# A hybrid decoder layer on one core: the attention projection of the second token half moved into the last attention units, and the output projection begun with that half

## The chip, the cores and the metric

The kernel runs on one core of one Trainium2 chip. The metric is the device time of one execution in microseconds (us), a median of three runs. The core has a matrix engine (TensorE, PE in the profile), a vector engine (VectorE, DVE), an engine for activation functions (ScalarE, ACT), a general engine (GpSimd, POOL) and SyncE (SP), which here issues nearly all DMAs. Each engine carries out its own list of instructions in order; an instruction that waits holds up everything behind it on that engine.

## What is computed

One decoder layer over 1024 tokens of width 1024, in fp32. Cut to the part that the change touches:

```python
h = rmsnorm(x); hp = h @ w_in                          # s5 inputs, q, k, v, gates
y_ssm = s5_mixer(...)                                  # ends in a GLU
y_nsa = nsa_mixer(...)                                 # compressed + selected + window attention
gate = sigmoid(hp[..., o4:].reshape(b, s, 2, D_MODEL))
merged = gate[..., 0, :] * (y_ssm @ w_proj_ssm) + gate[..., 1, :] * (y_nsa @ w_proj_nsa)
x = x + merged @ w_out
h2 = rmsnorm(x)
x = x + square(relu(h2 @ w_up)) @ w_down               # MLP, d_ff 4096
```

## The kernel before, in words

Every large product is made in three matmuls: both operands are split into a high and a low part (h and l), and high times high, low times high and high times low are summed in PSUM (`mm3`, lines 76 to 78). A split is one ACT instruction for the high part and one DVE or POOL instruction for the low part. Data lie with channels in the 128 partitions and tokens along a row. Tokens are worked in two halves of 512, and a product of 512 input channels for one block of 128 output channels and one half is 12 matmuls of 128x512.

The work in order of time: input projection and state-space mixer (to about 440 us of the span), attention (440 to 771), the projection `pB` of the attention output (775 to 833), the output projection `wo` (833 to 914), then the MLP: 16 rounds of up products, each made of seven smaller ones (B11, T2, B21, T3, T1, B22, T4), and four groups of down products from about 1250.

**Attention.** There are 16 units: for head group 0 the query blocks 0 to 7 of 128 tokens, then for group 1 the blocks 7 down to 0. So the second token half (512 to 1023) is complete for all heads when unit 11 (counted from 0) has stored its output. A unit makes scores (`sS`, `sW`), a softmax spread over DVE, ACT and POOL, transposes of the probabilities (`ptp`), and value products (`op`); its output `ot` is stored to DRAM (`oD`). The scores of a unit are interleaved with the values of the unit before.

**Filler.** A generator, `glu_fill`, makes the gated linear unit of the other mixer (`gps`) and its projection (`pA`) in small steps of three matmuls, 104 steps for both token halves. `step_fill` runs 0.55 of such a step for each value step (`FILL`), and a whole one in the last two units. Each projected row is scaled by its gate (`ga`, loaded from `gD`) and stored to `pD` (lines 783 to 787). The filler's temporary tiles come from `g_tile`, which has two buffers for all names; its product takes one of the two PSUM tiles `S` that the scores use too.

**Tail.** After the last unit the attention pools are closed. O, the attention output of both halves, is loaded from `oD` (`os`) and split (`Oh`, `Ol`). For each of the two halves and 8 blocks, pB = 12 matmuls; the gate `gb` (tanh on ACT) scales it (one DVE instruction), `pa`, the row that the filler had stored, is added (another), and the sum is split into `Mh`, `Ml`. Then `wo`: for each of 8 output blocks, in the order 0, 4, 1, 5, 2, 6, 3, 7, 48 matmuls for both halves.

**Memory.** A pool of 40 buffers (B) and one of 16 (W) hold the operands of the tail and of the MLP. `big_tile` hands out W for the tiles numbered 16 to 31 (of each 56), which are M rows 0 to 3 and later the MLP operands T3 and T1. The raw down weights (`wd`, line 1229, 16 loads) are put in W too, so in the last up round they wait until T3 and T1 were read.

**What sets the order.** The framework orders each engine's instructions itself, by a timeline of its own, from the order in which the code states them; each buffer's reuse waits for its last reader.

Of the kernel before, what the change touches and what calls it, by code (L numbers as in the profile page):

```python
# [8 lines left out]
F32 = mybir.dt.float32  # L9
F32R = mybir.dt.float32r  # L10
I32 = mybir.dt.int32
AF = mybir.ActivationFunctionType
# [15 lines left out]
FILL = 0.55  # L28
# [10 lines left out]
def hybrid_block(ctx: ExitStack, tc: tile.TileContext, A, out):  # L39
# [749 lines left out]

    last = proj_tok(wa, 1, 0)  # L790
# [16 lines left out]
    fill = glu_fill()  # L807
    early = [6]
# [175 lines left out]
    for n, (g, i) in enumerate(order):  # L984
        due[1] = FILL if n < 14 else 1.0
        if g == 0 and i >= 3:
            next(pk, None)
            next(pk, None)
        if n + 2 < 16:
            load_q(n + 2)  # L990
        va = unit_scores(*order[n + 1], Ks[order[n + 1][0]]) if n + 1 < 16 else None
        vb = unit_values(st)
        st = interleave(va, 6, vb, i + 1 + min(i + 1, 5) + 2)
# [20 lines left out]
    def big_tile(name):  # L1014

        nbig[0] += 1
        return (wd_tile if 16 <= (nbig[0] - 1) % 56 < 32 else op_tile)(name)
# [89 lines left out]
    t1es = ExitStack()  # L1107
    t1p = pool("t1", t1es, side="right")
    PAIRS = [0, 4, 1, 5, 2, 6, 3, 7]
    Oh, Ol = big_rows("O", 4)  # L1110
    wpn = [ring.raw(A["wpn"][m]) for m in range(2)]
    for hf in (1, 0):
        for m0 in (0, 2):
            os_ = T_tile("os")
            for j, sl in enumerate(HALVES):
                SP.dma_start(out=os_[:, sl], in_=oD[m0 + j, :, HALVES[hf]])
                split(Oh[m0 + j][hf], Ol[m0 + j][hf], os_[:, sl], lo_eng=DVE)
    Mh, Ml = big_rows("M", 8)
    for m0 in (0, 4):
        ws = []  # L1120
        for hf in (1, 0):
            sl = HALVES[hf]
            for m in range(m0, m0 + 4):
                if hf:
                    ws.append(ring.blocks(wpn.pop(0) if wpn else ring.raw(A["wpn"][m])))
                pa = t1p.tile([128, 512], F32, tag="pa", bufs=4, name="pa")
                SP.dma_start(out=pa, in_=pD[m][:, sl])
                gb = t1p.tile([128, 512], F32, tag="gb", bufs=4, name="gb")
                SP.dma_start(out=gb, in_=gD[8 + m][:, sl])
                act(gb, gb, AF.Tanh, scale=0.5)  # L1130
                ps = B_tile("pB")
                mm512(ps, ws[m - m0], [t[hf] for t in Oh], [t[hf] for t in Ol], True, True)
                stt(gb, gb, 1.0, ps, ALU.add, ALU.mult)
                tt(DVE, gb, gb, pa, ALU.add)
                split(Mh[m][hf], Ml[m][hf], gb, lo_eng=DVE)
    t1es.close()

# [9 lines left out]
    NG = 16  # L1147

    H2.alloc(3)
    for n, m in enumerate(PAIRS):  # L1150
        SP.dma_start(out=X2[m], in_=A["xT"][m * 128:(m + 1) * 128, :])
        w = [ring.weights(half(A["wo"][m], i)) for i in range(2)]
        if n % 2:
            ps = [B_tile("wo") for _ in range(2)]
        else:
            s_ = S_tile("wo")
            ps = [s_[:, sl] for sl in HALVES]
        for i, hf in ((0, 1), (1, 1), (0, 0), (1, 0)) if n == 0 else ((0, 1), (0, 0), (1, 1), (1, 0)):
            mm512(ps[hf], w[i], [t[hf] for t in Mh[4 * i:4 * i + 4]], [t[hf] for t in Ml[4 * i:4 * i + 4]], i == 0, i == 1)
        for hf in (1, 0):  # L1160
# [9 lines left out]
            act(o[:, sl], o[:, sl], scale=g2[:, m:m + 1])  # L1170
        if m == 3:
            H2.operands(3, X2[3], X2[7], H2.NAMES[:1])
        elif m > 3:
            H2.operands(m - 4, X2[m - 4], X2[m], H2.NAMES[m == 7:3])
# [281 lines left out]
```

## Time and profile before

| what | value |
|---|---|
| device time, median of 3 runs | 1571.67 us (1571.4 to 1574.04) |
| profiled execution: its own time, and its span | 1577.54 us, 1575.8 us |
| busy share of PE, DVE, ACT, POOL | 93%, 73%, 44%, 60% |
| granted PE clock, mean over the span | 0.97 |
| attention's last value product ends | 770.95 us |
| first matmul of pB, of wo, of the MLP | 774.82, 832.99 (steady), 914.36 us |

The span runs from the first to the last instruction; the 1.7 us around it belong to the execution's own time. PE is busy nearly throughout, so its idle stretches and the stretches at a lower clock are where time can be found; the last part of the attention and the start of the down projection are two of them.

### The profile page before, as it was taken

What the parts mean: (1) busy time and instruction counts of PE and PEld (TensorE: products, weight loads), DVE (VectorE), ACT (ScalarE), POOL (GpSimd) and SP (SyncE); (2) the same over time, 40 slices, a digit from 0 to 9 for tenths busy, and PEclk for the clock granted to TensorE, in tenths of its full rate; (3) what the DMA queues carried; (4) which work ended last, traced back from release to release, by engine and by line L of the source; (5) the groups of instructions that cost most, each with busy time, mean ns of one, the idle gap of its engine ahead of it and who ended that gap; (6) DMA issues with size and microseconds to landing.
All of it is one profiled execution on the core that took longest, in us unless ns stands there. A gap on an engine that the chain in (4) does not pass through costs nothing. (4 is left out here: it accounts for less than half of the span.)

```text
span 1575.8 us, 21400 instructions
## 1 busy us (share of the span) xinstructions
PE 1463.9 (93%) x7222; PEld 1220.7 (77%) x7222; DVE 1148.9 (73%) x1799; ACT 685.9 (44%) x1399; POOL 943.6 (60%) x825
## 2 busy tenths in 40 slices
PE   8689889999988999999799988999999889999999
PEld 6578878788886887888578867888888667787877
DVE  6356777632268788887574498987778999998965
ACT  6143442312157778878544452222222344444431
POOL 2564555433135544645223477998888668989883
PEclk9889999999989999999899999999999999999999
DMA  8654523344111222122565215332232342423202
GB/s 287 68 150 140 143 83 102 108 147 143 67 48 47 75 80 64 32 66 72 183 217 212 95 66 201 130 111 107 108 117 78 120 141 80 134 81 127 74 1 107
DMA packets 111103, 173.80 MB, mean 110 GB/s; under 512 B 23425, under 2 KB 44673, under 8 KB 110994
## 3 DMA queue, kind: packets, MB, share of 16 engines
q1 hardware_dynamic: 110994, 172.44, 34.6%
q8 instruction: 57, 0.93, 0.3%
q14 instruction: 52, 0.43, 0.1%
HBM read 124.15 MB, written 46.22 MB: 108 GB/s over the span
## 5 line engine op out<-in xcount | busy, mean ns | idle before, releaser
L81 POOL TENSOR_TENSOR wl<-raw,wh 128x512 fp32r<-128x512 f32 x128 | 184.6, 1450 | 169.7 <-ACT wh L96 165.7
L81 POOL TENSOR_TENSOR wl<-wd,wh 128x512 fp32r<-128x512 f32 x96 | 147.1, 1543 | 52.6 <-ACT wh L96 43.9
L96 ACT ACTIVATE wh<-raw 128x512 fp32r<-128x512 f32 x128 | 80.4, 629 | 164.3 <-PE wB L77 77.6
L96 ACT ACTIVATE wh<-wd 128x512 fp32r<-128x512 f32 x96 | 59.5, 626 | 112.8 <-POOL wd L81 42.0
L90 POOL TENSOR_SCALAR pS<-pS,rs 128x128 f32<-128x128 f32 (+7 forms) x64 | 48.3, 755 | 99.4 <-DVE rs L81 77.3
L76 PE MATMUL gt<-hTh,wmh 128*128 128x512 f32 x256 | 101.5, 397 | 0.0
L77 PE MATMUL gt<-hTl,wmh 128*128 128x512 f32 x256 | 101.3, 396 | 0.0
L78 PE MATMUL gt<-hTh,wml 128*128 128x512 f32 x256 | 101.2, 395 | 0.0
L81 DVE TENSOR_TENSOR pl<-ptp,ph 128x512 fp32r<-128x512 f32 x132 | 88.8, 686 | 14.5 <-ACT ph L96 13.5
L81 DVE TENSOR_TENSOR rr<-rr,rs 128x512 f32<-128x512 f32 x64 | 92.4, 1449 | 1.7
L96 ACT ACTIVATE ph<-ptp 128x512 fp32r<-128x512 f32 (+1 forms) x148 | 84.1, 587 | 14.8 <-PE ptp L900 14.0
L81 POOL TENSOR_TENSOR wl<-sum,wh 128x512 fp32r<-128x512 f32 x48 | 75.2, 1571 | 14.9 <-ACT wh L96 14.9
L81 POOL TENSOR_TENSOR wd<-wd 128x512 f32<-128x512 f32 x48 | 76.0, 1590 | 6.8 <-DMA wd<-in_wdn 5.5
L81 DVE TENSOR_TENSOR gt<-gt,rbc 128x512 f32<-128x512 f32 x32 | 22.0, 688 | 70.2 <-PE gt L78 63.7
L93 DVE SCALAR_TENSOR_TENSOR rr<-rr 128x512 f32<-128x512 f32 x64 | 71.3, 1117 | 1.8
L81 DVE TENSOR_TENSOR rr<-wT,rr 128x512 f32<-128x512 f32 x80 | 54.5, 684 | 21.8 <-PE wT L78 21.2
L96 ACT ACTIVATE wh<-sum 128x512 fp32r<-128x512 f32 x48 | 30.1, 629 | 89.3 <-PE wT L77 27.2
L96 ACT ACTIVATE pW<-pW,mx 128x64 f32<-128x64 f32 (+5 forms) x128 | 65.4, 515 | 4.2 <-DVE mx L855 4.0
L90 POOL TENSOR_SCALAR pW<-pW,rs 128x64 f32<-128x64 f32 (+5 forms) x128 | 65.4, 525 | 0.0
L891 PE MATMUL op<-ph,vs 128*128 128x512 f32 x132 | 61.2, 464 | 1.7 <-ACT ph L96 1.4
L81 POOL TENSOR_TENSOR wml<-wmr,wmh 128x512 fp32r<-128x512 f32 x32 | 42.9, 1346 | 28.2 <-ACT wmh L96 26.8
L893 PE MATMUL op<-pl,vs 128*128 128x512 f32 x132 | 55.7, 422 | 4.4 <-DVE pl L81 4.4
(626 smaller groups left out, 5077.1 us busy)
## 6 DMA issues: line engine op xcount, KB each, us to landing
raw<-in_wup SPq DMA_DIRECT2D x68, 256.0 KB, 2.6
wd<-in_wdn SPq DMA_DIRECT2D x64, 256.0 KB, 2.8
hD<-rr SPq DMA_DIRECT2D x26, 512.0 KB, 2.7
ru<-hD SPq DMA_DIRECT2D x18, 512.0 KB, 3.6
wmr<-in_wm SPq DMA_DIRECT2D x32, 256.0 KB, 3.0
gD<-gt SPq DMA_DIRECT2D x32, 256.0 KB, 2.1
xt<-in_x SPq DMA_DIRECT2D x16, 256.0 KB, 5.4
qkvD<-rw SPq DMA_DIRECT2D x32, 128.0 KB, 2.0
```

What stands on the lines that cost most here:

```text
L76: PE.matmul(out=o, lhsT=lh, rhs=rh, start=first, stop=False)
L77: PE.matmul(out=o, lhsT=lh, rhs=rl, start=False, stop=False)
L78: PE.matmul(out=o, lhsT=ll, rhs=rh, start=False, stop=last)
L81: e.tensor_tensor(out=o, in0=a, in1=b, op=op)
L90: e.tensor_scalar(out=o, in0=a, scalar1=s1, scalar2=s2, op0=op0, op1=op1)
L93: DVE.scalar_tensor_tensor(out=o, in0=a, scalar=s, in1=b, op0=op0, op1=op1)
L96: ACT.activation(out=o, in_=i, func=func, **kw)
L891: PE.matmul(out=op, lhsT=vv, rhs=ph, start=n == 0, stop=n == len(jobs) - 1)
L893: PE.matmul(out=op, lhsT=vv, rhs=pl, start=False, stop=False)
```

## The change

The filler goes on after its 104 steps, by 36 more: from unit 12 on it loads O of the second half (`os`), splits it (`Yh`, `Yl`), makes the 8 pB products of that half, scales them, adds the row of `pD` (`pa`) and stores the sum to `pD` again. So that it gets there, `FILL` goes from 0.55 to 0.75, and in units 12 to 15 1.4 steps run for each value step (`FILL2`). The tail loads the merged rows of the second half from `pD` (`mg`) and splits them, makes `wo` of that half for the blocks 0, 4, 1 and 5 around the 8 pB products of the first half, then `wo` of the first half for these four with weights that it kept, then the other four blocks for both halves. pB is 192 matmuls and wo 384, as before. The kept weights lie in W, and `big_tile` gives W to T2 and B21 in place of T3 and T1. Eight pieces of pB weights are loaded and split a second time.

```diff
@@ -25,7 +25,8 @@
 NH = 8
 NBC = dict(b=2, c=2)
 PERIOD = 6
-FILL = 0.55
+FILL = 0.75
+FILL2 = 1.4
 PB = 9
 CY = 4
 ATT = dict(op=("o", 1), b=("p", 3), c=("p", 3))
@@ -787,6 +788,29 @@
                 SP.dma_start(out=pD[m][:, sl], in_=ga)
                 yield
 
+        while not half1:
+            yield
+        wn = ring.weights(A["wpn"][0])
+        Yh, Yl = rows(glp, "Y", 4)
+        for m in range(4):
+            os_ = g_tile("os")
+            SP.dma_start(out=os_, in_=oD[m, :, sl])
+            split(Yh[m], Yl[m], os_, lo_eng=DVE)
+            yield
+        for m in range(8):
+            w = wn
+            if m < 7:
+                wn = ring.weights(A["wpn"][m + 1])
+            gb, pa = g_tile("gb"), g_tile("pa")
+            SP.dma_start(out=gb, in_=gD[8 + m][:, sl])
+            SP.dma_start(out=pa, in_=pD[m][:, sl])
+            act(gb, gb, AF.Tanh, scale=0.5)
+            ps = yield from prod("pB", w, Yh, Yl)
+            stt(gb, gb, 1.0, ps, ALU.add, ALU.mult)
+            tt(DVE, gb, gb, pa, ALU.add)
+            SP.dma_start(out=pD[m][:, sl], in_=gb)
+            yield
+
     last = proj_tok(wa, 1, 0)
     while active:
         bg()
@@ -982,7 +1007,9 @@
     for _ in range(5):
         st = next(va)
     for n, (g, i) in enumerate(order):
-        due[1] = FILL if n < 14 else 1.0
+        if n == 12:
+            half1.append(n)
+            due[1] = FILL2
         if g == 0 and i >= 3:
             next(pk, None)
             next(pk, None)
@@ -1014,7 +1041,7 @@
     def big_tile(name):
 
         nbig[0] += 1
-        return (wd_tile if 16 <= (nbig[0] - 1) % 56 < 32 else op_tile)(name)
+        return (wd_tile if 48 <= nbig[0] - 1 < 64 else op_tile)(name)
 
     def big_rows(name, n):
 
@@ -1104,37 +1131,7 @@
...
-    t1es = ExitStack()
-    t1p = pool("t1", t1es, side="right")
     PAIRS = [0, 4, 1, 5, 2, 6, 3, 7]
-    Oh, Ol = big_rows("O", 4)
-    wpn = [ring.raw(A["wpn"][m]) for m in range(2)]
-    for hf in (1, 0):
-        for m0 in (0, 2):
-            os_ = T_tile("os")
-            for j, sl in enumerate(HALVES):
-                SP.dma_start(out=os_[:, sl], in_=oD[m0 + j, :, HALVES[hf]])
-                split(Oh[m0 + j][hf], Ol[m0 + j][hf], os_[:, sl], lo_eng=DVE)
-    Mh, Ml = big_rows("M", 8)
-    for m0 in (0, 4):
-        ws = []
-        for hf in (1, 0):
-            sl = HALVES[hf]
-            for m in range(m0, m0 + 4):
-                if hf:
-                    ws.append(ring.blocks(wpn.pop(0) if wpn else ring.raw(A["wpn"][m])))
-                pa = t1p.tile([128, 512], F32, tag="pa", bufs=4, name="pa")
-                SP.dma_start(out=pa, in_=pD[m][:, sl])
-                gb = t1p.tile([128, 512], F32, tag="gb", bufs=4, name="gb")
-                SP.dma_start(out=gb, in_=gD[8 + m][:, sl])
-                act(gb, gb, AF.Tanh, scale=0.5)
-                ps = B_tile("pB")
-                mm512(ps, ws[m - m0], [t[hf] for t in Oh], [t[hf] for t in Ol], True, True)
-                stt(gb, gb, 1.0, ps, ALU.add, ALU.mult)
-                tt(DVE, gb, gb, pa, ALU.add)
-                split(Mh[m][hf], Ml[m][hf], gb, lo_eng=DVE)
-    t1es.close()
...
-    H2.alloc(3)
-    for n, m in enumerate(PAIRS):
-        SP.dma_start(out=X2[m], in_=A["xT"][m * 128:(m + 1) * 128, :])
-        w = [ring.weights(half(A["wo"][m], i)) for i in range(2)]
-        if n % 2:
-            ps = [B_tile("wo") for _ in range(2)]
-        else:
-            s_ = S_tile("wo")
-            ps = [s_[:, sl] for sl in HALVES]
-        for i, hf in ((0, 1), (1, 1), (0, 0), (1, 0)) if n == 0 else ((0, 1), (0, 0), (1, 1), (1, 0)):
-            mm512(ps[hf], w[i], [t[hf] for t in Mh[4 * i:4 * i + 4]], [t[hf] for t in Ml[4 * i:4 * i + 4]], i == 0, i == 1)
+    t1es = ExitStack()
+    t1p = pool("t1", t1es, side="right")
+    Oh, Ol = ([big_tile("O" + x) for _ in range(4)] for x in "hl")
+    Mh, Ml = big_rows("M", 8)
+
+    def wo_weights(m, keep):
+
+        w = []
+        for i in range(2):
+            t = ring.raw(half(A["wo"][m], i))
+            if not keep:
+                w.append(ring.blocks(t))
+                continue
+            h, l = wd_tile("woh"), wd_tile("wol")
+            split(h, l, t)
+            w.append(tuple(a[:].rearrange("p (k m) -> p k m", k=4) for a in (h, l)))
+        return w
+
+    def wo_mm(o, w, hf):
+        for i in range(2):
+            mm512(o, w[i], [t[hf] for t in Mh[4 * i:4 * i + 4]], [t[hf] for t in Ml[4 * i:4 * i + 4]], i == 0, i == 1)
+
+    def wo_out(m, hfs, ps):
+
+        for hf in hfs:
             o, sl = X2[m], HALVES[hf]
...
+    def merge(m, ps):
+
+        sl = HALVES[0]
+        pa = t1p.tile([128, 512], F32, tag="pa", bufs=2, name="pa")
+        gb = t1p.tile([128, 512], F32, tag="gb", bufs=2, name="gb")
+        SP.dma_start(out=pa, in_=pD[m][:, sl])
+        SP.dma_start(out=gb, in_=gD[8 + m][:, sl])
+        act(gb, gb, AF.Tanh, scale=0.5)
+        yield
+        stt(gb, gb, 1.0, ps(), ALU.add, ALU.mult)
+        tt(DVE, gb, gb, pa, ALU.add)
+        split(Mh[m][0], Ml[m][0], gb, lo_eng=DVE)
+
+    kept = {PAIRS[0]: wo_weights(PAIRS[0], True)}
+    for m in range(8):
+        if m % 2 == 0:
+            mg = T_tile("mg")
+        t = mg[:, HALVES[m % 2]]
+        SP.dma_start(out=t, in_=pD[m][:, HALVES[1]])
+        split(Mh[m][1], Ml[m][1], t, lo_eng=DVE)
+
+    def first_half(ms):
+
+        s_ = S_tile("wo")
+        for j, m in enumerate(ms):
+            SP.dma_start(out=X2[m], in_=A["xT"][m * 128:(m + 1) * 128, :])
+            if m not in kept:
+                kept[m] = wo_weights(m, True)
+            o = s_[:, HALVES[j]]
+            wo_mm(o, kept[m], 1)
+            wo_out(m, (1,), {1: o})
+
+    first_half(PAIRS[:2])
+    for m0 in (0, 2):
+        os_ = T_tile("os")
+        for j, sl in enumerate(HALVES):
+            SP.dma_start(out=os_[:, sl], in_=oD[m0 + j, :, HALVES[0]])
+            split(Oh[m0 + j], Ol[m0 + j], os_[:, sl], lo_eng=DVE)
+    first_half(PAIRS[2:3])
+    for m in range(8):
+        w = ring.weights(A["wpn"][m])
+        ps = B_tile("pB")
+        mg = merge(m, lambda: ps)
+        next(mg)
+        mm512(ps, w, Oh, Ol, True, True)
+        for _ in mg:
+            pass
+    first_half(PAIRS[3:4])
+    t1es.close()
+
+    for n, m in enumerate(PAIRS):
+        if n == 4:
+            H2.alloc(3)
+        if n < 4:
+            ps = {0: B_tile("wo")}
+            wo_mm(ps[0], kept[m], 0)
+            wo_out(m, (0,), ps)
+            continue
+        SP.dma_start(out=X2[m], in_=A["xT"][m * 128:(m + 1) * 128, :])
+        w = wo_weights(m, False)
+        if n % 2:
+            ps = [B_tile("wo") for _ in range(2)]
+        else:
+            s_ = S_tile("wo")
+            ps = [s_[:, sl] for sl in HALVES]
+        for i, hf in ((0, 1), (0, 0), (1, 1), (1, 0)):
+            mm512(ps[hf], w[i], [t[hf] for t in Mh[4 * i:4 * i + 4]], [t[hf] for t in Ml[4 * i:4 * i + 4]], i == 0, i == 1)
+        wo_out(m, (1, 0), ps)
         if m == 3:
             H2.operands(3, X2[3], X2[7], H2.NAMES[:1])
-        elif m > 3:
-            H2.operands(m - 4, X2[m - 4], X2[m], H2.NAMES[m == 7:3])
+        else:
+            for k in (0, 1) if m == 2 else (m - 4,):
+                H2.operands(k, X2[k], X2[k + 4], H2.NAMES[m == 7:3])
     pre = H2.first([A["wup"][j] for j in range(4)])
     H2.alloc(4)
     for n in H2.NAMES[3:]:
```

Three places show how the instructions move. The first is PE at the end of the attention. Before, the last filler product (`pA`) stands ahead of the last unit's transposes (`ptp`) and value products (`op`):

```order
L76 MATMUL pA_8059<-Gh_6523,wh_7998 128x512
L77 MATMUL pA_8059<-Gl_6527,wh_7998 128x512
L78 MATMUL pA_8059<-Gh_6523,wl_7997 128x512
L900 MATMUL ptp_8008<-c_ident_487,pS_7929 128x128
L900 MATMUL ptp_8020<-c_ident_487,pW_7930 128x128
L900 MATMUL ptp_8008<-c_ident_487,pS_7969 128x128
L900 MATMUL ptp_8020<-c_ident_487,pW_7970 128x128
L900 MATMUL ptp_8032<-c_ident_487,pW_7930 64x128
L900 MATMUL ptp_8032<-c_ident_487,pW_7970 64x128
L891 MATMUL op_7994<-ph_8013,vs0_4662 128x512
L893 MATMUL op_7994<-pl_8014,vs0_4662 128x512
```

In the changed kernel the last filler product is the eighth `pB`. The last two scores (`sS`, `sW`) of the last unit come behind it:

```order
L79 MATMUL pB_8235<-Yh_7517,wl_8107 128x512
L918 MATMUL op_8061<-pl_8181,vs1_4689 128x512
L845 MATMUL sS_8241<-kh0_4684,qT_8072 128x128
L846 MATMUL sS_8241<-kl0_4686,qT_8072 128x128
L925 MATMUL ptp_8268<-c_ident_487,pS_8120 128x128
L925 MATMUL ptp_8286<-c_ident_487,pW_8121 128x128
L925 MATMUL ptp_8268<-c_ident_487,pS_8150 128x128
L925 MATMUL ptp_8286<-c_ident_487,pW_8151 128x128
L916 MATMUL op_8061<-ph_8216,Vc_123 128x512
L925 MATMUL ptp_8295<-c_ident_487,pW_8121 64x128
L925 MATMUL ptp_8295<-c_ident_487,pW_8151 64x128
L845 MATMUL sW_8246<-kh1_4685,qT_8072 128x128
```

So the last scores, which stood ahead of the last filler products, now follow the last one, and no filler follows them.

The second is SP in the same stretch. Before, each filler product has one load (`ga`) and one store (`pD`):

```order
L707 DMA raw_7995<-in_wps 128x512
L783 DMA ga_8001<-gD_88 128x512
L916 DMA oD_83<-ot_7573 128x2x128
L787 DMA pD_87<-ga_7853 128x512
L783 DMA ga_8056<-gD_88 128x512
L916 DMA oD_83<-ot_7777 128x2x128
L787 DMA pD_87<-ga_8001 128x512
L916 DMA oD_83<-ot_7958 128x2x128
L787 DMA pD_87<-ga_8056 128x512
```

Now each has two loads (`gb`, `pa`) and one store, and with two buffers in `g_tile` the load of a `pa` follows the store of the row before:

```order
L805 DMA gb_7586<-gD_88 128x512
L806 DMA pa_7587<-pD_87 128x512
L811 DMA pD_87<-gb_7586 128x512
L805 DMA gb_7686<-gD_88 128x512
L708 DMA raw_7764<-in_wpn 128x512
L806 DMA pa_7687<-pD_87 128x512
L941 DMA oD_83<-ot_7758 128x2x128
L811 DMA pD_87<-gb_7686 128x512
L805 DMA gb_7770<-gD_88 128x512
L708 DMA raw_7846<-in_wpn 128x512
L806 DMA pa_7771<-pD_87 128x512
L811 DMA pD_87<-gb_7770 128x512
```

The load `pa_7687` takes the buffer of `gb_7586`, whose store stands three rows ahead of it; the load `gb_7686` takes that of `pa_7587`.

The third is the end of the attention on PE. Before, pB of both halves follows the last value product:

```order
L891 MATMUL op_7994<-ph_8013,vs0_4662 128x512
L893 MATMUL op_7994<-pl_8014,vs0_4662 128x512
L891 MATMUL op_7994<-ph_8025,vs1_4663 128x512
L893 MATMUL op_7994<-pl_8026,vs1_4663 128x512
L891 MATMUL op_7994<-ph_8037,Vc_123 128x512
L76 MATMUL pB_8190<-Oh_8102,wh_8182 128x512
L76 MATMUL pB_8216<-Oh_8102,wh_8208 128x512
L77 MATMUL pB_8190<-Ol_8104,wh_8182 128x512
```

Now it is the output projection of the second half, with kept weights (`woh`, `wol`):

```order
L916 MATMUL op_8264<-ph_8291,vs1_4689 128x512
L918 MATMUL op_8264<-pl_8292,vs1_4689 128x512
L916 MATMUL op_8264<-ph_8300,Vc_123 128x512
L77 MATMUL wo_8437<-Mh_8366,woh_8399 128x512
L78 MATMUL wo_8437<-Ml_8368,woh_8399 128x512
L79 MATMUL wo_8437<-Mh_8366,wol_8400 128x512
L77 MATMUL wo_8437<-Mh_8370,woh_8399 128x512
L78 MATMUL wo_8437<-Ml_8372,woh_8399 128x512
```

The first work after the attention thus reads merged rows (`Mh`, `Ml`), not O.

## Rows read from the trace of the kernel before

**Rows 1.** The page, part 1: busy time, share of the span, instructions.

```profile
PE 1463.9 (93%) x7222; PEld 1220.7 (77%) x7222; DVE 1148.9 (73%) x1799; ACT 685.9 (44%) x1399; POOL 943.6 (60%) x825
```

**Rows 2.** Windows: stretch, its length, busy time by engine, PE clock, DMA.

```profile
440.00:540.00 100.00, 87.17 (x498) 75.15 (x496) 76.53 (x233) 72.64 (x204) 50.03 (x78) 0.90 0.18 54
540.00:705.00 165.00, 160.08 (x950) 135.34 (x948) 142.73 (x320) 134.53 (x304) 88.22 (x107) 1.00 0.21 61
728.40:772.70 44.30, 38.47 (x224) 31.09 (x222) 29.98 (x100) 30.79 (x96) 15.38 (x34) 0.99 0.23 72
772.70:790.00 17.30, 12.60 (x38) 9.32 (x39) 9.81 (x14) 10.79 (x18) 5.89 (x5) 0.72 1.01 341
790.00:835.00 45.00, 43.44 (x190) 35.30 (x189) 32.00 (x42) 19.41 (x33) 12.11 (x9) 1.00 0.57 187
```

**Rows 3.** Timeline, SP: store of unit 11. Start, length, engine, line, operation.

```profile
728.42 0.37 SPq L916 DMA_DIRECT2D oD<-ot  x1
```

**Rows 4.** Timeline, PE: attention's last products, first pB and slow matmuls after it.

```profile
759.76 0.50 PE L76 MATMUL pA<-Gh,wh 128*128 128x512 f32 x1 [1.84 <-DVE mx L855]
...
766.83 0.27 PE L900 MATMUL ptp<-c_ident,pS 128*128 128x128 f32 x1
...
770.45 0.50 PE L891 MATMUL op<-ph,Vc 128*128 128x512 f32 x1 [0.22 <-DVE ph L81]
774.82 1.22 PE L76 MATMUL pB<-Oh,wh 128*128 128x512 f32 x2 [3.87 <-ACT Oh L96]
...
776.27 0.63 PE L78 MATMUL pB<-Oh,wl 128*128 128x512 f32 x1
...
778.40 0.62 PE L77 MATMUL pB<-Ol,wh 128*128 128x512 f32 x1
```

**Rows 5.** Timeline, PE: output projection in full stride, and the MLP's first product.

```profile
832.99 0.39 PE L77 MATMUL wo<-Ml,wh 128*128 128x512 f32 x1
...
835.94 0.39 PE L78 MATMUL wo<-Mh,wl 128*128 128x512 f32 x1
...
914.36 0.39 PE L76 MATMUL first<-B11h,wh 128*128 128x512 f32 x1
```

**Rows 6.** DMA issues, 690 to 772 us: count, KB each, median us to landing.

```profile
pD<-ga SPq DMA_DIRECT2D x7, 256.0 KB, 2.3
ga<-gD SPq DMA_DIRECT2D x6, 256.0 KB, 3.0
...
oD<-ot SPq DMA_DIRECT2D x6, 128.0 KB, 1.8
os<-oD SPq DMA_DIRECT2D x3, 256.0 KB, 4.4
```

**Rows 7.** Tile ga: its DMAs' times to landing over the whole span.

```profile
DMA to landing us min/median/max: 2.0/2.5/4.3
```

**Rows 8.** Timeline, ACT: tanh and high half; queue wait in brackets.

```profile
757.30 0.63 ACT L96 ACTIVATE ga<-ga 128x512 f32<-128x512 f32 x1 [1.96 <-DMA ga<-gD]
...
770.99 0.77 ACT L96 ACTIVATE ot<-op 64x256 f32<-64x256 f32 x2 [2.02 <-PE op L891]
```

**Rows 9.** Timeline, DVE: last window maximum, product with gate, value sum.

```profile
760.60 0.28 DVE L855 CUSTOM_DVE_ANT_0 pW<-sW,c_wbias 128x128 f32<-128x128 f32 x1
...
762.86 0.69 DVE L93 SCALAR_TENSOR_TENSOR ga<-ga,pA 128x512 f32<-128x512 f32 x1 [0.24 <-PE pA L78]
```

**Rows 10.** Timeline, POOL: last scaling of probabilities.

```profile
763.83 0.95 POOL L90 TENSOR_SCALAR pW<-pW,rs 128x128 f32<-128x128 f32 x3
```

**Rows 11.** Waits of PE, 1227 to 1304 us: total, times, longest.

```profile
PE dn L76 <- ACT wh L96: 5.9, 1, 5.9
PE dnb L78 <- POOL wl L81: 5.6, 1, 5.6
```

**Rows 12.** Waits of POOL, 1220 to 1260 us.

```profile
POOL wd L81 <- DMA wd<-in_wdn: 3.4, 1, 3.4
```

**Rows 13.** Windows: the start of the down projection.

```profile
1253.00:1280.00 27.00, 18.55 (x63) 14.71 (x64) 27.00 (x21) 13.80 (x26) 22.70 (x15) 0.75 0.06 20
```

More of the change, by code (lines that the diff above doesn't have):

```diff
@@ L807, in hybrid_block @@
     fill = glu_fill()
+    half1 = []
     early = [6]
@@ L1147, in hybrid_block @@
     NG = 16
-    H2.alloc(3)
-    for n, m in enumerate(PAIRS):
-        SP.dma_start(out=X2[m], in_=A["xT"][m * 128:(m + 1) * 128, :])
-        w = [ring.weights(half(A["wo"][m], i)) for i in range(2)]
-        if n % 2:
-            ps = [B_tile("wo") for _ in range(2)]
-        else:
-            s_ = S_tile("wo")
-            ps = [s_[:, sl] for sl in HALVES]
-        for i, hf in ((0, 1), (1, 1), (0, 0), (1, 0)) if n == 0 else ((0, 1), (0, 0), (1, 1), (1, 0)):
-            mm512(ps[hf], w[i], [t[hf] for t in Mh[4 * i:4 * i + 4]], [t[hf] for t in Ml[4 * i:4 * i + 4]], i == 0, i == 1)
-        for hf in (1, 0):
+    t1es = ExitStack()
[18 more added lines that the diff above has]
+        for hf in hfs:
             o, sl = X2[m], HALVES[hf]
```

## The prediction

> **What bounds the kernel now.** I read the busy shares first: PE 93% of the span, DVE 73%, ACT 44% [rows 1]. So a change pays only where PE stands idle or slow, or where something else ends a stretch last. The table by stretches shows where that is. From 440 to 540 us PE is idle for 12.8 of 100 us and its clock is 0.90; from 540 to 705 it is idle for 4.9 of 165; in the last four units 5.8 of 44.3; in the transition 772.7 to 790, 4.7 of 17.3 at clock 0.72, with the DMA engines full (share 1.01) [rows 2]. The timeline of PE then shows what ends these waits: 3.87 us between the attention's last product and the first pB, which waits for a split of O, and after it matmuls 0.426 us apart (776.27 to 778.40, five steps) [rows 4], where steady ones are 0.227 apart (832.99 to 835.94, thirteen steps) [rows 5].
>
> Two marks cut the affected stretch: the store of unit 11 at 728.42, from which the second token half is complete [rows 3], and the MLP's first matmul at 914.36 [rows 5]. Between them lie 185.9 us.
>
> **Before unit 11's store.** The filler's 288 matmuls of gps and pA were 240 ahead of this store and 48 behind it; now all 288 are ahead, and six of pB: 54 more. At 0.227 that is 12.3 us of PE. Of the 54, 24 come in units 0 to 4, 5.4 us beside 12.8 us of idle time [rows 2]; I take them as hidden. The other 30 come where 4.9 us are idle in 165; I take 2.0 as hidden. **Term: +4.9 us.** Bounds: +12.3, if PE's gaps are waits for DVE that move along with it; -5, if all fits and half of the time that the 0.90 clock cost comes back (0.90 means 20 of 100 us at half speed, some 10 us of work).
>
> **From unit 11's store to the MLP.** Here 48 matmuls go and 90 of pB come, but I don't think that PE sets the end. Each of the eight products has two loads and a store, through two buffers. The load of a `pa` takes the buffer of the row before, whose store must have landed: store 2.3, load 3.0 [rows 6], the sum on DVE 0.69 (no row shows this sum; I take it from the product with the gate, also DVE on 128x512) [rows 9]. So one round takes 6.0 us. The first: store of O 1.8 and load 3.0 [rows 6], split 0.63 + 0.69, gate load 3.0 into a buffer that the split frees, tanh 0.63 [rows 8], product with the gate 0.69: 10.4 us after unit 11's store. From the first to the eighth product with the gate: 0.7 + 6 x 6.0 + (3.0 + 0.63 + 0.69) = 41.0. The product holds one of the two PSUM tiles that the scores use, so the last window score waits for the eighth: four score matmuls 0.9; from the window's maximum to POOL's last scaling 760.60 to 764.78, 4.2 [rows 9, 10]; from the transpose at 766.83 to the end of the last value product, 770.45 + 0.50, 4.1 [rows 4]. No filler is left to lie beside these 9.2 us. Sum 60.6.
>
> To this comes waiting in DVE's queue, where each sum stands in line with the softmax: DVE is busy 29.98 of 44.3 us with 100 instructions, share 0.68, 0.30 us each [rows 2]; as an estimate 0.68 / 0.32 x 0.30 = 0.64 per round, 4.5 for seven. The attention ends 65.1 us after unit 11's store; before it was 42.5 (770.95 - 728.42).
>
> Then 0.77 for the copy of the output [rows 8] and three splits on ACT ahead of the first `wo`, 2.7 in all (bounds 0.8 and the 4.4 of before). The tail keeps 480 of its 576 matmuls: 109.0 us. Before, it took 139.5 from the first pB to 914.36, 8.7 more than 576 x 0.227. Now `wo` of two blocks, 10.9 us, covers the loads of O, but the X2 loads, 4 MB, come ahead of them; I take 5.0 lost, between 1.6 (what is idle after 790 now [rows 2]) and 8.7. Sum 65.1 + 2.7 + 109.0 + 5.0 = 181.8. **Term: -4.1 us.** Bounds: -15 (first rival) and +12 (second).
>
> The weights split a second time cost nothing here: ACT is busy 30.8 and POOL 15.4 of 44.3 us in the last units [rows 2], and these become longer. If ACT's share were not covered, 8 x 0.63 = 5.0.
>
> **At the start of the down projection.** The down weights wait for T2 and B21, in place of T3 and T1: two products of 12 matmuls earlier, 5.4 us. POOL waits 3.4 us there for such a load [rows 12], and PE 5.6 and 5.9 for splits behind it [rows 11]. But DVE is busy 27.0 of 27 us there [rows 13], so most of what PE gains may be given back. **Term: -2.7**, half of 5.4. Bounds -5.4, and +2 if the loads meet the last round's transfers.
>
> **Sum.** +4.9 - 4.1 - 2.7 = -1.9 us: no change that can be told (under 0.2%, 3.1 us, a measurement of this kernel can't tell). The profiled execution took 1577.54, which would become 1575.6; on the runs' median, 5.9 lower, 1569.8, say 1570.
>
> **A rule against it.** After 3.87 us of idle PE ran at the lower level, 1.2 GHz [rows 4]; after 1.84 us at 759.76 [rows 4] it did not, clock 0.99 over the last units [rows 2]. My sum has some 17 us idle there (65.1 less 48 of work), in eight gaps of about 2 us, and takes 2.4 GHz for granted. The Trainium skill, "TensorE: Matmul & The Clock Gate", "HAM oscillation — how this bites in real kernels", says that a kernel whose every tile's compute is shorter than the wait for its next data falls back to the slow clock at each tile. By that rule the sum would be that of the fourth rival below. The row of 1.84 us speaks against it, that of 3.87 us for it.
>
> **Rivals.**
> First, the chain of loads is hidden and PE sets the end. PE's work in the last units is 38.5 less 10.9 for the 48 matmuls, 27.6; with 90 x 0.227 = 20.4 and the 5.8 idle of before, 53.8 in place of 65.1. That is 11.3 less: -13.2 in all, 1558.5. It needs rounds of under 4.9 us with the queue; the fastest load took 2.0 [rows 7], so 2.3 + 2.0 + 0.69 just misses it. For it: loads of the gate are issued a round ahead, and I may have put the last score too strictly behind the eighth product.
>
> Second, the chain is longer. The slowest load of `ga` took 4.3 [rows 7] and loads of O 4.4 [rows 6]. Seven rounds with 1.3 more are 9.1, the first load 1.4: +8.6 in all, 1580. The place is the last four units, where scores wait for PSUM. It decides from 6.9 us a round on (6.64 is mine with the queue); from 7.4 the change is measurably slower.
>
> Third, nothing of the 54 earlier matmuls is hidden: 7.4 more, +5.5, 1577. For it: DVE and ACT are busy 76 and 73% from 440 to 540 [rows 2], so a unit may simply end later. Against it: they are not full.
>
> Fourth, the clock falls in the eight gaps. At 0.426 ten matmuls cost 2.0 us more, sixteen for eight gaps; PE's 17 us of idle time hide three quarters, so +4; with the tail's loss at 8.7 and 1 us in the last value products, +9 on the sum: +7, 1579.
>
> **Chances.** The forecast's case 0.38 (1564 to 1577), the first rival 0.27, second 0.19, third 0.11, fourth 0.05. Faster by over 0.2%: 0.13 of the forecast's case and 0.25 of the first rival, 0.38. Slower: 0.08 of the forecast's, 0.16, 0.09 and 0.04 of the others, 0.37. The rest, 0.25, is no change. The range reaches to the first rival at 1557, and to the second with part of the third at 1586.
>
> **What would show it.** The store of unit 11 near 733 (+4.9); the stores of `gb` about 6.6 us apart, and the SP queue's loads of `pa` behind them; PE waiting for DVE's product with the gate at scores of the last units; the last value product near 798, no pB between the scores and it; first `wo` 2.7 us later; the MLP's first matmul near 915; the two waits of PE at the down projection shorter by some 3 us in sum. It would be wrong if the stores come under 5 us apart or over 7.4, if unit 11's store moves by over 10 us or not at all, or if the down projection gives over 5 us.

## The result, and the profile after

The changed kernel takes 1588.52 us (median of 4, 1584.87 to 1592.69) against 1572.24 (median of 4): a ratio of 1.0107, 95% interval 1.0079 to 1.0135. It is slower; the forecast was no change, 1570, with a range up to 1586. Its profiled execution took 1584.87 us, span 1583.1. That is only 7.3 us more than the span before, since the stretch ahead of the attention, which the change doesn't touch, happened to be 8.5 us shorter in it (first score at 435.6 us in place of 444.1). So stretches are compared here from mark to mark.

The windows of the changed kernel (stretch, length, busy time of PE, PEld, DVE, ACT, POOL, granted clock, DMA share, GB/s) answer to [rows 2]:

```profile
440.00:540.00 100.00, 88.81 (x499) 75.45 (x498) 81.48 (x246) 78.76 (x219) 57.59 (x88) 0.93 0.21 68
540.00:705.00 165.00, 161.03 (x943) 136.31 (x941) 137.52 (x297) 129.13 (x285) 86.82 (x102) 1.00 0.25 78
723.80:792.10 68.30, 58.23 (x290) 45.43 (x290) 46.77 (x130) 40.90 (x116) 25.66 (x44) 0.93 0.42 141
792.10:815.00 22.90, 12.47 (x34) 7.29 (x35) 8.24 (x9) 9.86 (x19) 8.28 (x6) 0.70 1.03 395
815.00:919.80 104.80, 102.48 (x447) 83.50 (x448) 62.17 (x76) 49.20 (x82) 43.88 (x31) 1.00 0.40 138
```

The denser filler hardly changes the first two rows. The last four units now take 68.3 us (42.5 before), and 10 of them PE is idle. Worst is the fourth row: in the first 23 us of the tail PE works for 12.5, at clock 0.70, while the DMA engines are full.

The clock of the third row, 0.93, comes from two places. One is the end of the attention, below. The other is the third and fourth of the eight products: after a wait of 1.64 us PE starts the third, and soon its matmuls are 0.43 us apart. PE's timeline, and the window around:

```profile
739.87 0.50 PE L77 MATMUL pB<-Yh,wh 128*128 128x512 f32 x1 [1.64 <-DVE mx L880]
...
743.09 0.63 PE L77 MATMUL pB<-Yh,wh 128*128 128x512 f32 x1
743.52 0.63 PE L78 MATMUL pB<-Yl,wh 128*128 128x512 f32 x1
```

```profile
740.00:750.00 10.00, 8.32 (x27) 6.39 (x28) 5.27 (x12) 5.08 (x15) 3.51 (x3) 0.71 0.42 141
```

SP's timeline (start, length, engine, line, operation) gives unit 11's store [rows 3] and the first, second and last stores of the merged rows:

```profile
723.82 0.37 SPq L941 DMA_DIRECT2D oD<-ot  x1
...
736.13 0.32 SPq L811 DMA_DIRECT2D pD<-gb  x1
...
742.87 0.32 SPq L811 DMA_DIRECT2D pD<-gb  x1
...
784.88 0.32 SPq L811 DMA_DIRECT2D pD<-gb  x1
```

Eight stores lie 48.75 us apart, 7.0 a round. PE's timeline at the end of the attention (in brackets the wait ahead and what ended it) answers to [rows 4, 5]:

```profile
784.72 0.28 PE L890 MATMUL sW<-kcl,qT 128*128 128x64 f32 x1
787.48 0.33 PE L925 MATMUL ptp<-c_ident,pS 128*128 128x128 f32 x1 [2.48 <-POOL pS L91]
...
791.42 0.66 PE L916 MATMUL op<-ph,Vc 128*128 128x512 f32 x1
794.11 0.50 PE L77 MATMUL wo<-Mh,woh 128*128 128x512 f32 x1 [2.03 <-ACT Mh L97]
...
805.63 0.80 PE L77 MATMUL wo<-Mh,woh 128*128 128x512 f32 x1 [7.23 <-ACT Mh L97]
...
919.86 0.39 PE L77 MATMUL first<-B11h,wh 128*128 128x512 f32 x1
```

After six `wo` matmuls PE waits 7.23 us for a split of a merged row on ACT. ACT's timeline there, and after it SP's, show why:

```profile
797.01 0.63 ACT L97 ACTIVATE woh<-raw 128x512 fp32r<-128x512 f32 x1 [1.91 <-DMA raw<-in_wo]
804.43 0.63 ACT L97 ACTIVATE gb<-gb 128x512 f32<-128x512 f32 x1 [6.79 <-DMA gb<-gD]
804.97 0.61 ACT L97 ACTIVATE Mh<-mg 128x512 fp32r<-128x512 f32 x1
```

```profile
793.71 1.61 SPq L1206 DMA_DIRECT2D x<-in_xT  x3
...
797.66 0.33 SPq L1187 DMA_DIRECT2D gb<-gD  x1
```

The split stands behind the tanh of a gate that only a later product needs, and this gate's load stands behind three X2 loads of 512 KB.

At the start of the down projection PE's waits, 1215 to 1330 us, answer to [rows 11]:

```profile
PE dn L77 <- DVE acc L82: 9.6, 1, 9.6
PE dnb L77 <- DVE acc L82: 5.7, 3, 2.8
```

The two waits for weights are gone, and PE waits for DVE in their place. The weights were loaded earlier, as SP's timeline shows: the 16 loads begin 18.4 us ahead of the first down matmul (1239.29 us), where it was 9.0 before. The next group's loads `ru` follow later, behind four raw rows of hidden values:

```profile
1220.89 11.96 SPq L1308 DMA_DIRECT2D wd<-in_wdn  x16
1233.18 50.85 SPq L708 DMA_DIRECT2D raw<-hD  x4
1285.43 1.52 SPq L1315 DMA_DIRECT2D ru<-hD  x3
```

In the kernel before, two raw rows stood there:

```profile
1227.63 10.65 SPq L1229 DMA_DIRECT2D wd<-in_wdn  x16
1273.27 4.94 SPq L707 DMA_DIRECT2D raw<-hD  x2
1279.58 3.72 SPq L1236 DMA_DIRECT2D ru<-hD  x3
```

Against the first down matmul `ru` is 46.1 us later, 43.0 before. Against the MLP's first matmul it is the same, 365.6 and 365.2. Which of the two matters is a question for the experiments.

### The profile page after: what moved, and what is told of

It is laid out like the page before. It is cut to its first block, busy times and chain, and to the rows that moved or that the text cites. A ratio compares the mean times of both kernels' runs of the same rounds, so it can differ in the third digit from the quotient of the medians.

```text
span 1583.1 us, 21410 instructions
## 1 busy us (share of the span) xinstructions
PE 1470.2 (93%) x7222; PEld 1219.5 (77%) x7222; DVE 1159.1 (73%) x1799; ACT 689.5 (44%) x1407; POOL 956.6 (60%) x833
## 5 line engine op out<-in xcount | busy, mean ns | idle before, releaser
L82 POOL TENSOR_TENSOR wl<-wd,wh 128x512 fp32r<-128x512 f32 x96 | 143.2, 1503 | 63.3 <-ACT wh L97 60.5
L880 DVE CUSTOM_DVE_ANT_0 pS<-sS,c_cbias 128x128 f32<-128x128 f32 (+7 forms) x64 | 48.0, 750 | 16.0 <-PE sS L846 13.0
```

The costliest lines, as they stand in the source:

```text
L82: e.tensor_tensor(out=o, in0=a, in1=b, op=op)
L880: DVE.tensor_tensor_reduce(out=dst, in0=ps, in1=bias, scale=nsl, scalar=3e38, op0=ALU.add, op1=ALU.min, accum_out=mx[:, b, h:h + 1])
```

## The experiments

All stand against the kernel before, run beside them. The marks, from PE's and SP's timelines: the first score, unit 11's store, the end of the last value product, the first matmul of the tail (pB before, `wo` after), the MLP's first matmul, the first down matmul, the 97th of `dnb` (a sum of the down products; that matmul lies in the second of their four groups), and the end. Times in us; ratio of the whole to the kernel before.

| kernel | score to store 11 | to last value | tail's first to MLP | down to 97th dnb | MLP to end | ratio (95%) |
|---|---|---|---|---|---|---|
| before | 284.3 | 42.5 | 139.5 | 124.4 | 661.4 | 1 |
| changed | 288.2 | 68.3 | 125.8 | 128.4 | 663.2 | 1.0107 (1.0079 to 1.0135) |
| e1_fill75 | 289.0 | 33.1 | 135.4 | 124.5 | 661.7 | 1.0007 (0.9996 to 1.0019) |
| e2_pa_own | 290.2 | 65.1 | 124.3 | 126.7 | 661.3 | 1.0093 (1.0074 to 1.0112) |
| e3_tail_late | 290.0 | 70.1 | 114.2 | 126.2 | 661.2 | 1.0063 (1.0047 to 1.0078) |
| e4_w_t3t1 | 288.4 | 68.2 | 127.4 | 124.9 | 665.0 | 1.0134 (1.0113 to 1.0154) |
| e5_bank | 291.9 | 57.2 | 119.8 | 126.6 | 663.0 | 1.0061 (1.0036 to 1.0086) |
| e6_own_tail | 296.9 | 62.0 | 113.9 | 126.9 | 663.5 | 1.0071 (1.0047 to 1.0094) |
| e7_combo | 294.8 | 51.2 | 115.3 | 126.6 | 664.7 | 1.0013 (0.9997 to 1.0029) |
| e8_fill2_08 | 290.7 | 57.8 | 119.1 | 125.9 | 660.8 | 1.0125 (1.0090 to 1.0160) |
| e9_ru_first | - | - | - | - | - | 1.0183 (1.0161 to 1.0205) |
| e10_combo_ru | 297.6 | 55.5 | 114.8 | 130.9 | 668.0 | 1.0062 (1.0046 to 1.0077) |
| e11_bank_tail_ru | 290.0 | 57.6 | 114.9 | 131.0 | 669.3 | 1.0079 (1.0058 to 1.0099) |
| e12_before_bank | 293.3 | 41.2 | 135.5 | 124.2 | 662.9 | 0.9991 (0.9974 to 1.0007) |
| e13_combo_all | 317.8 | 53.7 | 115.5 | 127.7 | 664.4 | 1.0066 (1.0046 to 1.0086) |

How far one profile can be trusted: e10 differs from e7 only in loads of the down projection, yet its first two columns sum to 353.1 against 346.0. Differences under about 7 us in them are not read as effects.

**e1_fill75: the denser filler alone.**

```diff
-FILL = 0.55
+FILL = 0.75
```

> The kernel before with FILL 0.75 in place of 0.55, nothing else: the filler of 104 steps is done by unit 11, and the last four units have none. From the first score to the store of unit 11 it was 284.3 us before and 288.3 in the changed kernel. Theory A: the denser filler alone costs these 4 us, so about 288 here; and the last four units lose their 48 filler matmuls, 10.9 us of PE, of which the softmax chain lets only a part be gained: from the store of unit 11 to the last value product 36 to 39 us in place of 42.5. In all -1 to +1 us. Rival: unit 11 is late in the changed kernel because the pB part (weights, loads of O, six matmuls) is already mixed in before its store; then 285 to 286 here and the whole is 3 to 5 us faster.

Unit 11's store moved as in the changed kernel (+4.7 and +3.9 us), and the last units took 33.1, less than theory A's 36 to 39. Most of the 9.4 us that they gained was given back at once: PE then stands still for 10 us (3.9 before), until O is loaded and split. The two rows are the last units and this gap:

```profile
728.50:761.70 33.20, 30.59 (x188) 23.89 (x188) 29.05 (x105) 30.51 (x98) 16.66 (x38) 1.00 0.17 56
761.70:771.80 10.10, 0.00 (x0) 0.00 (x0) 0.84 (x2) 4.76 (x10) 5.12 (x5) 0.65 0.84 278
```

**e2_pa_own: own buffers for pa.** In e6, e7, e10 and e13 `gb` has such buffers too (tag Gl).

```diff
-            gb, pa = g_tile("gb"), g_tile("pa")
+            gb = g_tile("gb")
+            pa = gg[0].tile([128, 512], F32R, tag="Gh", bufs=4, name="pa")[:].bitcast(F32)
```

> The changed kernel, with four buffers of their own for the filler's pa (in tiles that the other mixer's projection has left), so that its load no longer waits for the store of the row before; all else as it was. Theory A (the two buffers set the pace of the last units): the rounds of pB shrink from 7.0 us to 4 or less where nothing else holds them, and from the store of unit 11 to the last value product it takes 54 to 58 us in place of 68; the whole 8 to 13 us faster than the changed kernel. Rival B (the last units are long because the scores wait for PSUM tiles and for DVE, whatever the loads do): 65 to 68 us there, and no gain over 3 us.

65.1 us: rival B. The window answers to the third row of the changed kernel, with the same idle time of PE and the same clock:

```profile
728.90:794.00 65.10, 56.18 (x290) 44.55 (x290) 45.43 (x130) 40.26 (x116) 25.07 (x44) 0.94 0.42 137
```

**e3_tail_late: the tail's other loads held back.**

```diff
+            tt(POOL, X2[m][:, 0:1], Mh[7][1][:, 0:1].bitcast(F32), Ml[7][1][:, 0:1].bitcast(F32), ALU.add)
             SP.dma_start(out=X2[m], in_=A["xT"][m * 128:(m + 1) * 128, :])
...
+        tt(POOL, pa[:, 0:1], ...)   # and gb, ahead of their loads in merge
```

> The changed kernel, in whose tail the loads of X2 and of pa and gb are made to wait until the last merged row of the second half (Mh, Ml of block 7) is split, by writing one column of their buffers from it; all else as it was. Theory A: the wait of 7.2 us of PE after six wo matmuls comes from ACT, which stands at the tanh of a gb whose load is behind 1.5 MB of X2, with the merged rows' splits queued behind it; so that wait goes, and from the first wo matmul to the MLP's first it takes 115 to 118 us in place of 125.8, the whole 7 to 10 us faster than the changed kernel. Rival B: the DMA engines are full from 794 to 820 in any case, and what is put later makes the residual sums and pB late instead: 122 to 126 us, and waits of PE for DMA-fed splits further on.

Theory A's number, and a little better: the tail takes 114.2 in place of 125.8 us. ACT's order has no tanh in it until the merged rows are split:

```profile
804.85 0.63 ACT L97 ACTIVATE woh<-raw 128x512 fp32r<-128x512 f32 x1 [1.23 <-DMA raw<-in_wo]
805.38 0.61 ACT L97 ACTIVATE Mh<-mg 128x512 fp32r<-128x512 f32 x1
```

All kernels with this edit lie at 113.9 to 115.5. The DMA engines are just as busy; what they carry first has changed. So the edit moves the bytes and the order on ACT together. For the order speaks the trace of the changed kernel: six loads of merged rows (`mg`) were issued there by 790.72 and took 8.4 us at most, and ACT stood at the tanh until 804.43.

**e4_w_t3t1: the old rule for W.**

```diff
-        return (wd_tile if 48 <= nbig[0] - 1 < 64 else op_tile)(name)
+        return (wd_tile if 64 <= nbig[0] - 1 < 80 else op_tile)(name)
```

> The changed kernel with the W buffers given to T3 and T1 again, as before the change, in place of T2 and B21. Theory A: the earlier down weights are what costs time at the start of the down projection, since SP then has a third raw row of hidden values, whose buffer is not free, ahead of the loads ru that the next group needs: with the old rule ru is issued first again, and from the first down matmul to the end it takes 339 us as before the change, in place of 343.8; the 2.8 us that the up rounds gained, mostly right after the first product, are lost or not, and the MLP's second product may wait for rows of M, whose buffers T2 and B21 now take (2 to 10 us). Rival B: the 4.6 us there are a spread between executions: 343 us again.

The number of theory A came nearly: 340.2 us from the first down matmul to the end (339.2 before, 343.8 in the changed kernel), and SP again issues two raw rows and then `ru`:

```profile
1241.57 10.36 SPq L1308 DMA_DIRECT2D wd<-in_wdn  x16
1287.21 4.93 SPq L708 DMA_DIRECT2D raw<-hD  x2
1293.52 3.71 SPq L1315 DMA_DIRECT2D ru<-hD  x3
```

But the first down matmul stands 324.8 us after the MLP's first here (319.4 in the changed kernel, 322.2 before), so that from the MLP's first to the end it is 665.0, no less than 663.2. What is won at one mark had been lost at another; e9 and e10 tell what sets both.

**e5_bank: pB in another PSUM bank.**

```diff
-            ps = S_tile(name)[:, 0:512]
+            ps = B_tile(name) if name == "pB" else S_tile(name)[:, 0:512]
```

> The changed kernel, with the filler's pB products in one of the three PSUM banks of the transposes in place of one of the two tiles of the scores; all else as it was. Theory C (the scores of the next unit wait for the PSUM tile that a pB holds until DVE has taken it, and everything in order behind them on PE waits too): with two tiles free for scores, from the store of unit 11 to the last value product it takes 56 to 62 us in place of 68.3, and PE's waits at scores for DVE go. Theory A (the loads and the store of the filler in two buffers): 66 to 69 us. Rival D (transposes and value products now wait for PSUM in their turn): 66 to 72 us, with waits at the transposes.

57.2 us: theory C's number, though PE's waits at scores were only 2.1 us in the changed kernel (1.0 now), and 2.7 at pB itself for the scores' maximum on DVE (none now); most went by another way. The last scores' row of the tile view (first and last start), of the changed kernel, then of this one, and its window:

```profile
L890 PE MATMUL sW<-kcl,qT x11: 272/276/277, 724.9 to 784.7; 128*128 128x64 f32 x11
```

```profile
L890 PE MATMUL sW<-kcl,qT x9: 272/277/278, 733.9 to 772.6; 128*128 128x64 f32 x9
```

```profile
732.60:789.80 57.20, 52.00 (x284) 41.79 (x284) 40.94 (x122) 39.00 (x110) 24.79 (x44) 1.00 0.46 148
```

The last score ran 7.4 us before the last value product ended (792.1), and now 17.2 us before (789.8): the last softmax lies beside products again, and the clock stays at 2.4 GHz. Over the first two columns, the five kernels with pB in a tile of the scores (e8 apart) need 355.3 to 360.1 us (mean 357.5), the four with the bank (e13 apart) 346.0 to 353.1 (mean 349.0): 8.5 us. At this mark own buffers differ by nothing that shows: 355.3 and 358.9 with, 356.5, 356.6 and 360.1 without; with the bank 346.0 and 353.1 against 349.1 and 347.6. The five have a clock of 0.89 to 0.95 in the last units, the four 1.00 (e10: 0.94); how much of the 8.5 us is order and how much clock, no run separates.

At the first `wo` it is otherwise. In e5 each `gb` load goes out right behind the store of the row before, by SP's timeline; the eight stores lie 6.4 us apart (e11: 6.5, forecast 6.6), and DVE's wait at the product with the gate is for the tanh on ACT, not for PE:

```profile
783.76 0.32 SPq L811 DMA_DIRECT2D pD<-gb  x1
784.12 0.43 SPq L805 DMA_DIRECT2D gb<-gD  x1
...
790.00 0.32 SPq L811 DMA_DIRECT2D pD<-gb  x1
```

```profile
DVE gb L94 <- ACT gb L97: 2.0, 3, 1.2
```

The last store leaves at 790.00, the loads of the merged rows begin behind it at 793.47, and the first `wo` comes 9.0 us after the last value product (2.0 in the changed kernel):

```profile
798.78 0.80 PE L77 MATMUL wo<-Mh,woh 128*128 128x512 f32 x1 [8.97 <-ACT Mh L97]
```

In the changed kernel this product waited for both, and in e7, with the bank and own buffers, for PE alone, with the stores 5.0 us apart:

```profile
DVE gb L94 <- ACT gb L97: 4.0, 4, 2.0
DVE gb L94 <- PE pB L79: 2.1, 2, 1.3
```

```profile
DVE gb L94 <- PE pB L79: 3.8, 3, 1.5
```

So two limits of nearly the same length lie side by side, the two buffers and the tile. From the first score to the first `wo` the five kernels without the bank need 357.3 to 362.1 us (mean 359.5), the bank alone 358.1 and 356.7 (e5, e11), both parts 348.1 and 355.2 (e7, e10). That e5 is faster as a whole than the changed kernel comes, by the profiles, from its tail, 119.8.

**e6_own_tail and e7_combo: parts together.** e6 has own buffers for gb and pa and the edit of e3; e7 the bank of e5 too.

> The changed kernel with four buffers each for the filler's gb and pa, and the tail's X2, pa and gb loads held until the last merged row is split (as tried apart before: pa alone gave 3.2 us in the last units, the held loads 11.5 in the tail). Theory C: without any wait for a store the last units still take 60 to 64 us from the store of unit 11, since PSUM and the order on PE stay; the whole 1576 to 1579. Theory A: 54 to 57 us and 1569 to 1572.

> Everything together: pB in a PSUM bank of the transposes, own buffers for gb and pa, and the tail's other loads held until the last merged row is split. Theory C: neither PSUM nor a store holds the last units, so they come down to PE's own work of 46 us and the 9 us of the last softmax: 53 to 58 us; the whole 1566 to 1572, at or below the kernel before. If the waits only change their place (rival D): 60 us or more, and 1575.

e6: 62.0 us in the last units, as theory C had it, but 296.9 ahead of them, and the whole at 1581.45, above both forecasts. e7: 51.2 us and 1572.70: the loss is gone, but nothing is won against the kernel before. Against e6, which lacks only the bank, the medians differ by 8.8 us. Its last units and its tail:

```profile
734.40:785.60 51.20, 47.89 (x271) 39.36 (x269) 40.62 (x112) 33.64 (x97) 24.64 (x43) 1.00 0.48 151
785.60:902.90 117.30, 113.42 (x481) 91.84 (x481) 70.77 (x80) 58.29 (x99) 59.65 (x61) 0.96 0.56 196
```

PE is busy 161 of 168.5 us. Yet from the first score to the last value product e7 needs 346.0, and e1, the same filler without pB, 322.1: 23.9 us for 96 matmuls that are worth 21.8 in the tail.

**e8_fill2_08: fewer products among the last units.**

```diff
-FILL2 = 1.4
+FILL2 = 0.8
```

> The changed kernel with FILL2 0.8 in place of 1.4: some three of the eight pB products stand after the last unit's own work in the program, or beside its last softmax. Theory C (each product among the last units costs more than its 2.7 us, since scores wait behind it): from the store of unit 11 to the last value product 50 to 60 us, and the products left over lie beside the last softmax, so that the MLP's first product comes 4 to 10 us earlier against the store of unit 11 than in the changed kernel (196.0). Rival: the merged rows of the second half come that much later, the output projection waits for them, and nothing is gained: 194 to 200.

Half each: the last units took 57.8 us, as theory C had it, but the first `wo` came 16.4 us after them (2.0 in the changed kernel), and the MLP 193.3 after unit 11's store, between theory C's 186 to 192 and the rival's 194 to 200. The whole is no faster than the changed kernel.

**e9_ru_first, e10_combo_ru, e11_bank_tail_ru: `ru` ahead of the raw rows.** e9 is the changed kernel with this edit, e10 is e7 with it, e11 is e10 without own buffers. The later groups alone have it.

```diff
+                        tt(DVE, t[:, 0:1], u[0][:, 0:1], u[2][:, 0:1], ALU.add)   # t: raw row, u: loaded by ru
                         SP.dma_start(out=t, in_=hD[f + c * NG][:, sl])
```

> The changed kernel, in which the raw rows of hidden values for the later three groups of down products are loaded behind the group's loads ru (a column of their buffer is written from ru first), W as the change has it. Theory A (SP stands at a raw row whose buffer is not free, with ru behind it): from the first down matmul to the 97th of dnb it takes 121 to 125 us in place of 128.4 (124.4 before the change), and nothing else moves; the whole 3 to 7 us faster than the changed kernel. Rival E (DVE sets the pace there, which loads come first does not matter): 126 to 129.

> All four together: pB in a PSUM bank of the transposes, own buffers for gb and pa, the tail's other loads held back, and ru ahead of the raw rows. If the places found add up: from the first down matmul to the 97th of dnb 122 to 125 us in place of 126.6 without the last, from unit 11's store to the MLP as without it (168.5), and the whole 1567 to 1570, 0.1 to 0.3% faster than the kernel before. If the start of the down projection has only its wait moved: 1571 to 1574.

> The same without the own buffers: gb and pa share the two of the filler as in the changed kernel. Theory C (PSUM, the tail's order and the order of loads are the causes, the two buffers are not): from the first score to the last value product 346 to 351 us (349.1 with the bank alone, 346.0 with own buffers too), and the whole within 3 us of the run with own buffers. Theory A: 354 us or more there, and 6 us or more in all.

Theory A missed: 1.0183 for e9 (three executions; the fourth, the profiled one, took 2894 us and is not read, so that the place of e9's loss stays open), and 130.9 in e10, above rival E's 126 to 129 too. With no raw row ahead of it, `ru` still waits, for its own buffer, until 1276.25:

```profile
1276.25 2.62 SPq L1320 DMA_DIRECT2D ru<-hD  x3
...
1295.31 1.81 SPq L1332 DMA_DIRECT2D raw<-hD  x4
```

This is 44.9 us after the first down matmul, where e7, with the raw rows ahead, has 44.7. So SP's order was not what held. Both buffers are freed by DVE, which makes the operands, and DVE is busy throughout, as the third busy time of these windows shows, of the changed kernel (1215 to 1300) and of the kernel before (1210 to 1295):

```profile
1215.00:1300.00 85.00, 70.99 (x302) 57.01 (x301) 81.47 (x82) 30.69 (x56) 57.69 (x37) 0.94 0.34 122
```

```profile
1210.00:1295.00 85.00, 71.99 (x297) 58.00 (x296) 81.71 (x83) 31.08 (x57) 57.06 (x37) 0.92 0.36 122
```

That is rival E's cause: DVE sets the pace from the up rounds on. It rests on these rows, as no run makes DVE's work shorter. PE is ahead or behind by the weights, and meets DVE again at the second group. Late raw rows make it worse (668.0 and 669.3 to the end). e11 needs 347.6 us from the first score to the last value product, theory C's number. But the two buffers do cost something: the first `wo` comes 9.1 us after that (2.0 in e10), and the whole is 3.6 us above e10.

**e12_before_bank and e13_combo_all: the bank for the whole filler.** The edit of e5 for all products, in the kernel before and in e7.

```diff
-            ps = S_tile(name)[:, 0:512]
+            ps = B_tile(name)
```

> The kernel before the change, with all products of its filler (gps and pA) in a PSUM bank of the transposes in place of one of the two tiles of the scores; nothing else. Theory C (a filler product in a tile of the scores holds the next scores up, about 1 us a product as the eight pB showed): the kernel before pays it too, for 24 products; from the first score to the last value product 312 to 322 us in place of 326.8, the whole 4 to 12 us faster. Rival D (in units with more value work the transposes need their three banks, and wait in turn): 325 to 332 us, no gain or slower.

> The run with everything together but ru (pB's bank, own buffers, the tail's loads held back; 1572.7 us), with gps and pA in the transposes' banks too. Theory C: from the first score to the last value product 330 to 341 us in place of 346.0, and the whole 1560 to 1568, faster than both kernels. Rival D: 346 to 352 us, 1573 or more.

Theory C missed in both. The first scores come 15.4 us earlier than in the kernel before, and 12.8 earlier than in e7, so that the first column can't be compared. e12: 1569.26 us, ratio 0.9991 (0.9974 to 1.0007); e13: 1581.94, 1.0066 (1.0046 to 1.0086). The bank helps the eight products at the end, not the filler in general: it gains nothing in e12, and e13 is some 8 us slower than e7 by the ratios. That is rival D's outcome; that the transposes wait for their banks in turn is not shown. Of all kernels run, none is faster than the kernel before by more than its interval.

## Why the prediction was wrong, step by step

- **Before unit 11's store, +4.9.** Right: +3.9, and +4.7 with the filler's rate alone (e1).
- **Last units, 65.1 us.** Near in size (68.3), by half of its cause, so partly luck. The sign that I had named came, stores 7.0 us apart (6.6 forecast), but by itself it proved nothing: with own buffers the stretch stayed at 65.1 and 62.0 us (e2, e6). A second limit of the same length lay beside the two buffers, the PSUM tile; without it the attention ends some 8.5 us earlier (e5, e7, e10, e11). I had seen the tile, but only as the last link of the chain of loads. It sets the order on PE: the last scores have to come behind the last product, and so the last softmax lies bare. With the tile out of the way the forecast chain is what is left: rounds of 6.4 and 6.5 us, and a first `wo` 9 us behind the last value product (e5, e11).
- **First `wo` 2.7 us after.** Right: 2.0.
- **Tail, 5.0 us lost, between 1.6 and 8.7.** This step failed, and it is the largest: 125.75 less 480 x 0.227 are 16.8. I counted the X2 loads as bytes ahead of O, and thought of PE's `wo` as cover. What cost was, by the trace, ACT's order: a tanh for later work, whose load stood behind these bytes, held the splits that PE wanted at once. e3, which moves that tanh and the bytes, took back 11.6 of it. My upper bound was the loss of a tail that had another order on ACT.
- **Down projection, -2.7.** Failed: nothing was gained. The weights came earlier and PE's waits for them went, but from the MLP's first matmul to the end it takes 663.2 us against 661.4; all kernels without the `ru` edit have 660.8 to 665.0, with either rule for W. I had the row that says so, DVE busy 27.0 of 27 us, and took half of the gain against it.
- **The clock.** The fourth rival had 0.05. The Trainium skill's rule ("TensorE: Matmul & The Clock Gate", "HAM oscillation — how this bites in real kernels"), that a kernel whose every tile's compute is shorter than the wait for its next data falls back to the slow clock at each tile, the trace bears out in part only. No wait ahead of the eight products is as long as a product (1.64 us at most, against 2.7 for 12 matmuls), yet the clock fell at two of them, the third and fourth (0.71 from 740 to 750 us), and again from the bare softmax on (0.70 from 792 to 815). So a part of this rival came true, and my sum had nothing for it.
- **Sum.** +3.9 ahead of unit 11's store, +10.1 from it to the MLP (196.0 against 185.9), +1.8 in the MLP: 15.8, as the medians have it (16.3). Of the 17.7 us between this and the forecast's -1.9 the tail has 11.8, the down projection 4.5, the last units 3.2; the other two terms came out 1.7 better. The range was too narrow because the bounds of the tail came from rows of an order that the change replaced.

What stays open: why e6, e7 and e10 take 6.6 to 9.4 us more ahead of unit 11's store than the changed kernel. All three have own buffers for `gb` and `pa`, and issue the loads of four rows ahead of that store (704 to 712 us).

## What to carry to other kernels

Work moved into gaps costs little only if it doesn't reorder the engines that those gaps were waiting for: here the moved matmuls cost about their full time even in e7, 23.9 us for 21.8 by one profile each. Look at each in-order queue that the change rearranges, ACT's included, for an instruction of later work that stands ahead of one wanted now, and take the bound of a term from that queue, not from the loss that the old order had. And a forecast sign that two causes would both give, as the spacing of the stores, tells nothing; undo the cause. If the time then stays, a second limit may stand beside the first: undo both before you call either harmless, and look at the next mark too.

## What was unexpected

PE's matmuls ran at the lower clock after a wait of only 2.48 us (787.48), and even after one of 1.64 (739.87), where after 1.84 us before the change it had not fallen. So the length of a wait alone does not tell whether the clock falls. With the waits of 2.03 and 7.23 us behind the first of these the clock's mean from 792 to 815 us was 0.70. And taking the filler products earlier in the attention out of the tile of the scores gained nothing (e12).
